# A third block buffer, a mean square taken later, and a longer written order in a sliding-window attention layer

## The chip, the cores and the metric

One core of one Trainium2 chip runs the whole program. The metric is the device time of one execution in microseconds (us), the median of several runs. The core has five instruction streams that run side by side and meet only at semaphores: TensorE (PE; its weight loads are shown as PEld), VectorE (DVE), ScalarE (ACT), GpSimd (POOL) and SyncE (SP, which here only issues DMAs). POOL issues DMAs too, above all the ones that add to what lies at the destination.

## The reference

One layer for 512 tokens of width 2048, all in float32. A root-mean-square norm is followed by a sliding-window attention with 32 heads and its output projection; the result is added to `x`. Then a second norm of `x` feeds a gate, the gate scales an embedding, and a last norm makes the output.

```python
hn = rmsnorm(x, norm_g)
y = swa_mixer(hn, swa_w_in, swa_w_out, swa_sinks, rel_bias)
x = x + y                                        # the kernel's x1
emb = p @ ple_proj
g = jax.nn.sigmoid(rmsnorm(x, ple_norm) @ ple_gate)
x = x + emb * g
return rmsnorm(x, final_g)
# rmsnorm(x, g) = x * rsqrt(mean(x * x) + 1e-6) * g
```

## The kernel before

**Products.** A float32 product is made of three matmuls of a high and a low part (lines 126 to 128). So each block of weights of 128 x 1024 is loaded as `braw` or `grown`, ScalarE copies its high part into `bhi` (line 760), and VectorE subtracts to get the low part `blo` (line 761). Three buffers hold the high parts, three the low ones, and three the raw blocks (a fourth in the last stages). The raw buffer comes free when `blo` has been made, and only then SP's next load (line 752) may start.

**Two large products** follow the attention: the output projection (weights `w_out`, results into `x1`, the four column quarters of `x` after attention) and the gate (weights `ple_gate`). Each is done by a Strassen-like scheme of six large parts in the order 1, 7, 6, 5, 3, 4 (line 669) and some small ones (`smallo`, `smallg`). A part `p` has two halves `jj`, and a half has four steps `m`: 12 matmuls, then some later work, then `todo()` and `between()`. A place in the program is written (p, jj, step) here. The last part of the gate, 4, is written out by hand behind the loop.

**Weights that grow.** In the gate the blocks of parts 7, 6 and 4 share eight buffers `grown`. Each is loaded for part 7; POOL later adds a further block by an accumulating DMA (line 739, always behind the `blo` made from the old contents), which gives the block of part 6, and later that of part 4.

**Turning x1.** The gate's product needs `x1` transposed. Half of it goes over TensorE (`turn`, line 1030). The other half, columns j = 2 and 3 for two halves `th` of the tokens, goes over VectorE (`turn_blocks`, line 1048): two VectorE transposes of 32 x 32 squares into a tile `blocks` with tag "e" and two buffers, a POOL DMA of it to DRAM (`apart`, line 1057), four POOL DMAs that gather it back (line 1064), and four ScalarE instructions that scale it into `hT` (`scale_turned`, line 1066). `turns_at` (line 1075) says at which steps of part 4 of the projection and part 1 of the gate these come. There are four such blocks: (2,0), (3,0), (2,1), (3,1). In their order, the third takes the buffer of the first, and the fourth that of the second.

**The norm.** `squares(t, j)` (line 1025) has ScalarE square a quarter row of `x1`, with the sum kept in `ssq2` and the squares themselves thrown into the scratch tile `s2`. Four of the sixteen are issued where the quarter is complete; twelve are queued in `squares_due` and taken one for each `todo()` from (1,1,0) of the gate on, so that the last comes at (7,1,3). There VectorE sums them (line 1594) and scales the mean (line 1423), POOL raises it to the power -1/2 (line 1425, result `rstd2`), and ScalarE runs one Sigmoid on a single column, which brings in the table for the gates. `rstd2` is first used by `gated` (line 1451), which starts behind step (6,1,1).

**Order.** Inside `tc.manual_schedule(engines=...)` the engines named keep the order in which the program is written; for other engines a planner chooses the order from its own costs. TensorE and SP are always written. ScalarE is written from part 4 of the projection (line 1361) to `last_out.close()` (line 1412), which stands behind the first forms of the gate. In part 1 of the gate ScalarE, VectorE and POOL are the planner's; from part 7 on (line 1560) all engines are written.

Of the kernel before, what the change touches and what calls it, by code (L numbers as in the profile page):

```python
# [11 lines left out]
F32 = mybir.dt.float32  # L12
F32R = mybir.dt.float32r
AF = mybir.ActivationFunctionType
ALU = mybir.AluOpType
AX = mybir.AxisListType
# [4 lines left out]
P = 128  # L21
# [34 lines left out]
def trunk_kernel(ctx: ExitStack, tc: tile.TileContext, a: dict):  # L56
    nc = tc.nc

    def pool(name, bufs=1, **kw):
        return ctx.enter_context(tc.tile_pool(name=name, bufs=bufs, **kw))  # L60
# [25 lines left out]
    WE = 1024  # L86
# [71 lines left out]
    def run(gen):  # L158
        for _ in gen:
            pass  # L160
# [38 lines left out]
    for k in range(KC):  # L199
# [67 lines left out]
        f, e = k == 0, k == KC - 1  # L267
# [18 lines left out]
        for part in "hl" if f else "lh":  # L286
            for t in range(NB):
                c = slice(t * P, (t + 1) * P)
# [6 lines left out]
        if 3 <= k < 3 + NB:  # L295
            t = k - 3
# [104 lines left out]
    for b in range(exact, BUCKETS):  # L401
        d = np.nonzero(bk == b)[0]
        if len(d):
            lo, n = P - 1 + int(d.min()), len(d)
# [301 lines left out]
    for nm, p in SUMS:  # L706
        for q in (6, 5) if (nm, p) == ("ple_gate", 5) else (p,):
            sum_small(nm, q)
        for jj in range(2):
            for m in range(4):  # L710
                t = summed[nm, p, jj, m] = tc.dram_tile([P, WE], F32, name=f"{nm}_{p}_{jj}_{m}")
# [13 lines left out]
    class Pieces:  # L725
# [38 lines left out]
        def split_last(self, k, hi, lo):  # L764

            i = len(self.specs) - 8 + k
            raw = self.base.pop(i)
            nc.scalar.copy(hi, raw)
            nc.vector.tensor_sub(lo, raw, hi.bitcast(F32))
            self.made[i] = tuple([t[:, :512], t[:, 512:]] for t in (hi, lo))  # L770
# [135 lines left out]
    blocks = TWOS * UNITS  # L906
# [64 lines left out]
    late = pool("late", reuse_waits="tile")  # L971
    rooms.append(late)
    x1s = late.tile([P, 4, NB, 512], F32, name="x1s")
    x1 = [x1s[:, j] for j in range(4)]
    ssq2 = const.tile([P, NB, 4], F32, name="ssq2")
# [39 lines left out]
    def load_x(j, queue):  # L1015
        queue.dma_start(x1[j], a["x"].rearrange("(t p) d -> p t d", p=P)[:, :, j * 512 : (j + 1) * 512])

    def partial(nm):
        return late.tile([P, 2, 2, 512], F32, tag="partial", name=nm, bufs=3)

    s1, s2, s7 = partial("s1"), partial("s2"), partial("s7")

    squares_due = []

    def squares(t, j):
        nc.scalar.activation(s2[:, j % 2, t % 2], x1[j][:, t, :], AF.Square, accum_out=ssq2[:, t, j : j + 1])

    hT, swapped = {}, {}

# [17 lines left out]

    def turn_blocks(j, th):

        t = late.tile([P, WE], F32, tag="e", name=f"blocks{j}_{th}", bufs=2)  # L1050
        to = t.rearrange("p (a k t q) -> p t k a q", a=4, k=4, t=2)
        for tb in range(2):
            assert not missing[j, 2 * th + tb]
            src = x1[j][:, 2 * th + tb, :].rearrange("p (k a q) -> p k a q", k=4, a=4)
            nc.vector.transpose(to[:, tb], src)
        apart[j, th] = tc.dram_tile([P, WE], F32, name=f"apart{j}_{th}")
        nc.gpsimd.dma_start(apart[j, th], t)
# [25 lines left out]
    def turns_due(at):  # L1083
        for part, j, th in turns_at.get(at, ()):
            part(j, th)
# [272 lines left out]
    last_out = ExitStack()  # L1358
    for n, p in enumerate(ORDER_OUT):
# [7 lines left out]
        for jj in range(2):  # L1367
# [12 lines left out]
            def todo():  # L1380
                nonlocal fg
                step = next(calls)
                part = x_at.get((p, jj, step))
                if part is not None:
                    load_x(part, nc.sync)
                part = embed_steps.get((p, jj, step))
                if part is not None:
                    embedding.prepare(part)
                next(nxt, None)
                if p == 4:  # L1390
                    turns_due((p, jj, step))
                if (p, jj, step) == (4, 1, 1):
                    fg = late.tile([P, D], F32, tag="fg", name="fg")
                    nc.sync.dma_start(fg, a["final_g"].partition_broadcast(P))
                if (p, jj) == (4, 1):
                    for _ in range(2 if step >= 2 else 0):
                        turn(*turns.pop(0), "o")
                        next(ple_first, None)
# [10 lines left out]
        if p == 3:  # L1409
            turns = [(kp, 0) for kp in range(4)]  # L1410
    run(ple_first)
    last_out.close()
    assert not turns


    power = const.tile([P, NB], F32, name="power")
    nc.gpsimd.memset(power, -0.5)

    def power_of_mean(out, ssq, nm):

        w = out.shape[-1]
        ms = const.tile([P, NB], F32, tag="ms_r", name=f"ms_{nm}")[:, :w]
        nc.vector.tensor_scalar(ms, ssq, 1.0 / D, EPS, op0=ALU.mult, op1=ALU.add)
        yield
        nc.gpsimd.tensor_tensor(out, ms, power[:, :w], op=ALU.pow)

    rstd2 = const.tile([P, NB], F32, name="rstd2")
    ss2 = const.tile([P, NB], F32, tag="sums", name="ss2")
# [4 lines left out]
    def load_embeds(c, jj):  # L1433
        t = embed_of[c, jj] = late.tile([P, 2, 512], F32, tag="e", name=f"e{c}_{jj}", bufs=2)
        nc.sync.dma_start(t, embeds[c, jj])

    def embeds_for(of, which):
        return {t: embed_of[of, which][:, t % 2] for t in ((2, 3) if of == 5 else (0, 1))}
# [91 lines left out]
    def open_bank(jj, tb, tag, c=slice(0, 512)):  # L1530

        ps = opened[jj, tb, c.start] = bank(f"open{jj}_{tb}_{c.start}", tag)
        nc.scalar.mul(ps[:, c], s2[:, jj, tb, c], -1.0)
# [22 lines left out]

    for n, p in enumerate(ORDER_PLE[:-1]):
        if n == 1:

            ctx.enter_context(  # L1560
                tc.manual_schedule(
                    engines={getattr(mybir.EngineType, v) for v in ("PE", "SP", "DVE", "Activation", "Pool")}
                )
            )
        nxt = ple_forms.steps(ORDER_PLE[n + 1])
        for jj in range(2):
            calls = iter(range(4))

            def todo():
                step = next(calls)  # L1570
                k = early.get((p, jj, step))
                if (p, jj, step) in embed_loads:
                    load_embeds(*embed_loads[p, jj, step])
                while small_due:
                    small_due.pop(0)()
                if (p, jj, step) == (5, 0, 2):
                    assert len(moves) == 4
                    while moves:
                        moves.pop(0)()
                if (p, jj, step) == (5, 0, 3):  # L1580
                    for square in moved.pop(0):
                        square()
                if p == 1:
                    turns_due((p, jj, step))
                if turns:
                    turn(*turns.pop(0), "t")
                    return
                next(nxt, None)
                if p == 1:
                    next(nxt, None)  # L1590
                if squares_due:
                    squares_due.pop(0)()
                    if not squares_due:
                        nc.vector.tensor_reduce(ss2, ssq2, axis=AX.X, op=ALU.add)
                        run(power_of_mean(rstd2, ss2, "r2"))
                        nc.scalar.activation(ss2[:, :1], ss2[:, :1], AF.Sigmoid)
                if k is not None:
                    split_last(k)
                if (p, jj, step) in opens:
                    open_bank(*opens[p, jj, step])  # L1600

            def between(m, ps):
                if (p, m) == (7, 3):
                    gate(p, jj, ps, None)
                q = ple_steps.get((p, jj, m))
                if q is not None:
                    small_ple.prepare(q)
                for q in SMALL["ple_gate"].get((p, jj), {}).get(m, ()):
                    small_ple.product(q)
                if (p, jj, m) == (6, 1, 1):  # L1610
                    later.append(partial_of(gate_later, "sum", 0, None, embeds_for(1, 0)))

            ps = unit(p, jj, at_ple, ple_forms, todo, between)
            last_two, held_e = (p, jj) == (3, 1), {}
            if not (p == 7 or last_two):
                later.insert(0, partial_of(gate_later, p, jj, ps, held_e))
            for of, which in EMBEDS.get((p, jj), ()):
                e = embeds_for(of, which)
                held_e.update(e)
                if of == 1:  # L1620
                    later.insert(1, partial_of(gate_later, "sum", which, None, dict(e)))
                    held_e.clear()
            if p == 5:
                while moved:
                    later.extend(moved.pop(0))
        run(nxt)
# [4 lines left out]
    f = ple_forms.made[4]  # L1631
# [84 lines left out]
    n = done[3]  # L1716
# [81 lines left out]
```

## Time and profile before

| | |
|---|---|
| median of 3 runs | 787.8 us (787.77 to 787.85) |
| the profiled execution | 788.14 us, its span 786.4 us |
| TensorE busy | 773.9 us, 98% of the span |
| VectorE, ScalarE, GpSimd busy | 615.6, 528.8, 161.8 us |
| mean granted TensorE clock | 0.996 |
| DMA | 210.92 MB, mean 268 GB/s |

The span runs from the first to the last instruction; 1.74 us of the execution lie around it. A row of the timeline gives start, duration, engine, line, operation, what it writes and reads, and in square brackets how long the engine stood idle before it and what ended that. A row of the windows gives the stretch, its length, the busy time of PE, PEld, DVE, ACT and POOL with the number of instructions that start in it, the granted clock, the DMA engines' busy share (above 1 where transfers of two queues overlap) and GB/s. A row of the waits gives the total, the number and the longest of one kind of wait. A row of DMA issues gives the count, the size of one and the median time from issue to landing.

### The profile page before, as it was taken

The page shows a single profiled execution, that of the slowest core. Times are in us where ns is not written, and L with a number is a line of the kernel's source. Part 1 is how long each engine was busy: PE and PEld are TensorE (multiplying, and loading weights), DVE is VectorE, ACT ScalarE, POOL GpSimd, SP SyncE. Part 2 cuts the span into 40 slices and gives each one's busy share as a digit, 9 for nine tenths or more (in the row PEclk, how much of TensorE's full clock was granted, in tenths as well). Part 3 has the DMA queues.
Part 4 walks back from the last instruction along what each step waited for, and adds up shares of the span by engine and source line. Part 5 has one row for each costly group of instructions (what it writes and reads, how often), then busy time and mean ns, then how long its engine had stood idle before and what let it go on. Part 6 is the DMA issues. An engine that isn't in the chain of part 4 may idle for free.

```text
span 786.4 us, 11162 instructions
## 1 busy us (share of the span) xinstructions
PE 773.9 (98%) x3668; PEld 645.6 (82%) x3668; DVE 615.6 (78%) x1065; ACT 528.8 (67%) x1121; POOL 161.8 (21%) x293
## 2 busy tenths in 40 slices
PE   9999999999999999999999999999999999999995
PEld 8888888888888888888888888888887888887785
DVE  4537697877877688877878898976898879897996
ACT  6734586766767676766666654677675978865974
POOL 0201423132222314132222200001012102221111
PEclk9999999999999999999999999999999999999998
DMA  9988899999999989999997489868799999999956
GB/s 347 286 213 298 188 263 313 291 287 268 276 262 271 273 231 297 276 281 258 288 256 199 139 320 340 263 217 278 242 352 345 261 332 272 223 269 305 303 131 214
DMA packets 51738, 210.92 MB, mean 268 GB/s; under 512 B 7825, under 2 KB 8849, under 8 KB 45921
## 3 DMA queue, kind: packets, MB, share of 16 engines
q1 hardware_dynamic: 39152, 154.58, 56.4%
q0 software_dynamic: 12528, 55.64, 34.5%
q8 instruction: 29, 0.48, 0.2%
q14 instruction: 29, 0.23, 0.1%
HBM read 194.40 MB, written 77.65 MB: 346 GB/s over the span
## 4 chain that ended last, share of the span: by engine, by line
PE 80%; issue 10%; DMA 5%; DVE 3%; POOL 1%; ACT 1%; POOLq 0%; DVEq 0%; ACTq 0%
PE gps L126 7%; PE gps L127 7%; PE gps L128 7%; PE qps L126 7%; PE qps L128 7%; PE qps L127 7%; PE g L127 3%; PE o L127 3%; PE g L128 3%; PE o L126 3%; PE g L126 3%; PE o L128 3%; DMA braw<-ple_gate 3%; PE s L485 2%; DMA apart<-blocks 2%
## 5 line engine op out<-in xcount | busy, mean ns | idle before, releaser
L761 DVE TENSOR_TENSOR blo<-braw,bhi 128x1024 fp32r<-128x1024 f32 x100 | 121.3, 1219 | 24.1 <-ACT bhi L760 23.5
L760 ACT CAST bhi<-braw 128x1024 fp32r<-128x1024 f32 x100 | 105.2, 1053 | 51.2 <-PE o L128 16.5
L126 PE MATMUL gps<-xh,whi 128*128 128x512 f32 x256 | 100.0, 390 | 0.0
L127 PE MATMUL gps<-xl,whi 128*128 128x512 f32 x256 | 99.9, 390 | 0.0
L128 PE MATMUL gps<-xh,wlo 128*128 128x512 f32 x256 | 99.8, 390 | 0.0
L126 PE MATMUL qps<-xh,whi 128*128 128x512 f32 x224 | 87.8, 392 | 0.0
L128 PE MATMUL qps<-xh,wlo 128*128 128x512 f32 x224 | 87.5, 390 | 0.0
L127 PE MATMUL qps<-xl,whi 128*128 128x512 f32 x224 | 87.4, 390 | 0.0
L575 POOL TENSOR_SCALAR_AFFINE_SELECT own<-r 64x512 fp32r<-64x512 f32 (+1 forms) x48 | 32.5, 677 | 238.4 <-DVE r L565 224.4
L110 DVE TENSOR_TENSOR wlo<-wraw,whi 128x1024 fp32r<-128x1024 f32 x60 | 73.5, 1226 | 4.5 <-ACT whi L109 4.4
L126 PE MATMUL o<-bhi,fho 128*128 128x512 f32 x192 | 74.8, 390 | 0.0
L127 PE MATMUL o<-blo,fho 128*128 128x512 f32 x192 | 74.8, 390 | 0.0
L128 PE MATMUL o<-bhi,flo 128*128 128x512 f32 x192 | 74.7, 389 | 0.0
L109 ACT CAST whi<-wraw 128x1024 fp32r<-128x1024 f32 x60 | 62.3, 1040 | 6.3 <-issue 4.1
L127 PE MATMUL g<-blo,fhg 128*128 128x512 f32 x160 | 62.7, 392 | 1.2 <-DVE blo L761 1.2
L126 PE MATMUL g<-bhi,fhg 128*128 128x512 f32 x160 | 62.9, 393 | 0.5 <-ACT bhi L760 0.5
L128 PE MATMUL g<-bhi,flg 128*128 128x512 f32 x160 | 62.4, 390 | 0.0
L128 PEld LDWEIGHTS gps<-xh,wlo 128*128 128x128 f32 x256 | 48.1, 188 | 10.3
L126 PEld LDWEIGHTS gps<-xh,whi 128*128 128x128 f32 x256 | 48.1, 188 | 9.2
L529 ACT ACTIVATE t<-t,sm 128x129 f32<-128x129 f32 (+1 forms) x128 | 49.6, 390 | 8.7 <-DVE sm L525 7.4
L127 PEld LDWEIGHTS gps<-xl,whi 128*128 128x128 f32 x256 | 48.1, 188 | 8.8
L564 ACT CAST r<-pt 128x256 fp32r<-128x256 f32 x56 | 20.9, 372 | 49.8 <-PE pt L551 49.4
(295 smaller groups left out, 1826.2 us busy)
## 6 DMA issues: line engine op xcount, KB each, us to landing
wraw<-in_w_gate_in SPq DMA_DIRECT2D x32, 512.0 KB, 7.7
w_out<-in_w_out POOLq DMA_DIRECT2D x32, 512.0 KB, 9.1
braw<-w_out SPq DMA_DIRECT2D x32, 512.0 KB, 6.6
wraw<-in_w_q SPq DMA_DIRECT2D x28, 512.0 KB, 6.7
braw<-in_w_out SPq DMA_DIRECT2D x22, 512.0 KB, 5.5
braw<-in_ple_gate SPq DMA_DIRECT2D x22, 512.0 KB, 7.0
xw<-in_first SPq DMA_DIRECT2D x14, 640.5 KB, 6.6
w_out<-in_w_out SPq DMA_DIRECT2D x16, 512.0 KB, 10.7
```

The lines of the kernel that those rows point to most:

```text
L109: nc.scalar.copy(hi, raw)
L110: nc.vector.tensor_sub(lo, raw, hi.bitcast(F32))
L126: nc.tensor.matmul(ps, sh, mh, start=first, stop=False, skip_group_check=more)
L127: nc.tensor.matmul(ps, sh, ml, start=False, stop=False, skip_group_check=more)
L128: nc.tensor.matmul(ps, sl, mh, start=False, stop=last, skip_group_check=more)
L485: nc.tensor.matmul(s_ps[:, u, : 2 * n], st, of_keys[:, first * 2 * QB : (first * QB + n) * 2], start=True, stop=True)
L529: nc.scalar.activation(su, su, AF.Exp, bias=sm[:, u : u + 1], accum_out=sm[:, 2 + u : 3 + u])
L564: nc.scalar.copy(rh, src)
L575: nc.gpsimd.affine_select(out=flat(own), in_=flat(r).bitcast(F32), pattern=[[0, 8], [sign, HB]], compare_op=ALU.is_ge, fill=0.0, base=-HB ...
L760: nc.scalar.copy(hi[:, :n], raw)
L761: nc.vector.tensor_sub(lo[:, :n], raw, hi[:, :n].bitcast(F32))
```

## The change

Three edits go together. The third block (2,1) gets room of its own in the first half of the scratch tile `s2`; so that this half is free, all squares go to its second half. The queue of squares starts one step later, at (1,1,1), and takes two at (1,1,3); the sum and the mean move from (7,1,3) to (6,0,1), the power to (6,0,3), and the Sigmoid stays behind the last square but reads `power` in place of the sum. And `last_out.close()` moves behind part 1 of the gate, so that ScalarE's written order runs on through that part.

```diff
@@ squares, line 1025
+    root_due = None
+    ROOT_AT = (6, 0, 1), (6, 0, 3)
 
     def squares(t, j):
-        nc.scalar.activation(s2[:, j % 2, t % 2], x1[j][:, t, :], AF.Square, accum_out=ssq2[:, t, j : j + 1])
+        nc.scalar.activation(s2[:, 1, t % 2], x1[j][:, t, :], AF.Square, accum_out=ssq2[:, t, j : j + 1])
@@ turn_blocks, line 1048
-        t = late.tile([P, WE], F32, tag="e", name=f"blocks{j}_{th}", bufs=2)
+        if (j, th) == (2, 1):
+            t = s2[:, 0].rearrange("p n c -> p (n c)")
+        else:
+            t = late.tile([P, WE], F32, tag="e", name=f"blocks{j}_{th}", bufs=2)
@@ line 1412
     run(ple_first)
-    last_out.close()
@@ the gate's loop, line 1557
     for n, p in enumerate(ORDER_PLE[:-1]):
         if n == 1:
+            last_out.close()
@@ its todo()
-                if squares_due:
+                if (p, jj, step) == ROOT_AT[0]:
+                    assert not squares_due
+                    nc.vector.tensor_reduce(ss2, ssq2, axis=AX.X, op=ALU.add)
+                    root_due = power_of_mean(rstd2, ss2, "r2")
+                    next(root_due)
+                if (p, jj, step) == ROOT_AT[1]:
+                    run(root_due)
+                if squares_due and (p, jj, step) != (1, 1, 0):
                     squares_due.pop(0)()
+                    if (p, jj, step) == (1, 1, 3):
+                        squares_due.pop(0)()
                     if not squares_due:
-                        nc.vector.tensor_reduce(ss2, ssq2, axis=AX.X, op=ALU.add)
-                        run(power_of_mean(rstd2, ss2, "r2"))
-                        nc.scalar.activation(ss2[:, :1], ss2[:, :1], AF.Sigmoid)
+                        nc.scalar.activation(ss2[:, :1], power[:, :1], AF.Sigmoid)
```

More of the change, by code (lines that the diff above doesn't have):

```diff
@@ L1569, in todo @@
             def todo():
+                nonlocal root_due
                 step = next(calls)
```

## The prediction

> **What bounds the kernel now.** I read the page first, then TensorE's waits, then the timeline around each wait. The page says that TensorE sets the time:
>
> ```profile
> PE 773.9 (98%) x3668; PEld 645.6 (82%) x3668; DVE 615.6 (78%) x1065; ACT 528.8 (67%) x1121; POOL 161.8 (21%) x293
> PE smallo L127 <- DVE blo L761: 1.5, 1, 1.5
> PE g L127 <- DVE blo L761: 1.2, 2, 0.8
> PE g L126 <- ACT bhi L760: 0.5, 1, 0.5
> ```
>
> The waits of TensorE are few: one of 1.5 us in the projection and three in the gate. An edit pays only through these, or costs by making new ones. The windows place them and size them by matmul starts:
>
> ```profile
> 590.00:600.00 10.00, 10.00 (x46) 8.29 (x45) 9.79 (x13) 6.57 (x10) 1.05 (x2) 1.00 1.01 308
> 600.00:610.00 10.00, 8.49 (x38) 6.67 (x37) 7.10 (x9) 4.25 (x5) 4.50 (x9) 1.00 1.03 379
> 720.00:730.00 10.00, 8.36 (x33) 5.96 (x33) 8.30 (x11) 8.30 (x14) 1.76 (x2) 1.00 1.07 329
> ```
>
> An undisturbed stretch starts 46 matmuls in 10 us. The stretch from 600 starts 38: stall 1 costs 8/46 x 10 = 1.7 us. That from 720 starts 33: stall 2, with its small stumbles, costs 13/46 x 10 = 2.8 us. Together 4.5 us is all that can be won here.
>
> **Stall 1, and the third buffer.** The timeline around 600:
>
> ```profile
> 577.59 0.54 POOL L1057 DMA_DIRECT2D apart<-blocks  x1 [16.37 <-DVE blo L761]
> ...
> 596.01 0.56 POOL L1057 DMA_DIRECT2D apart<-blocks  x1 [7.47 <-DVE blocks L1055]
> 599.00 1.05 ACT L760 CAST bhi<-braw 128x1024 fp32r<-128x1024 f32 x1 [1.15 <-PE o L128]
> 599.14 0.65 DVE L1147 TENSOR_TENSOR small_alo<-small_sums_o,small_aho 128x512 fp32r<-128x512 f32 x1
> 602.88 0.39 PE L126 MATMUL smallo<-bhi,small_aho 128*128 128x512 f32 x1
> 602.90 0.71 DVE L1055 STREAM_TRANSPOSE blocks<-x1s 128x512 f32<-128x512 f32 x1 [3.11 <-DMA apart<-blocks]
> 603.54 2.32 DVE L761 TENSOR_TENSOR blo<-braw,bhi 128x1024 fp32r<-128x1024 f32 x2
> 604.78 0.50 PE L127 MATMUL smallo<-blo,small_aho 128*128 128x512 f32 x1 [1.51 <-DVE blo L761]
> ```
>
> VectorE stands 3.11 us at the fourth block's transpose, whose buffer is the second block's: that block's DMA, issued at 596.01, is still reading it. Behind the transpose two `blo` are queued, and TensorE, done with the high part at 602.88, needs the first of them. With the third block in `s2`, the fourth takes the first block's buffer. That one's DMA went out at 577.59, some 22 us before the buffer is wanted, against the 3.8 us (596.01 to 599.8) after which the second block's was not yet through. The wait goes. VectorE then transposes at 599.79 (599.14 + 0.65), is done at 600.43, and the `blo`, whose cast ended at 600.05, lasts until about 601.6. TensorE needs it at 602.88 + 0.23 = 603.11, so 1.5 us of margin are left and nothing takes the wait's place: the next thing that could be late is the second `blo`, done at 602.8. I count **-1.7 us**. The transpose, its two halves and its five DMAs stay the same in number.
>
> Does a gain at 604 last to the end? Everything behind is released by TensorE's or VectorE's progress, unless DMA is the limit throughout. It is not: see the idle shares below.
>
> **Stall 2, and the power that is taken later.** Here the loads are late:
>
> ```profile
> 719.57 1.05 ACT L760 CAST bhi<-braw 128x1024 fp32r<-128x1024 f32 x1 [2.86 <-DMA braw<-ple_gate]
> 725.92 1.05 ACT L760 CAST bhi<-braw 128x1024 fp32r<-128x1024 f32 x1 [0.65 <-DMA braw<-ple_gate]
> e<-embeds SPq DMA_DIRECT2D x1, 512.0 KB, 4.6
> braw<-ple_gate SPq DMA_DIRECT2D x1, 512.0 KB, 12.7
> 700.00:710.00 10.00, 10.00 (x46) 8.29 (x45) 8.22 (x10) 5.49 (x7) 3.00 (x4) 1.00 1.06 275
> ```
>
> ScalarE waits for `braw` before the casts that TensorE lacks. The DMA issues by short windows show why: a load of 512 KB issued between 676 and 678 lands in 4.6 us, one issued between 712 and 714 in 12.7 us, with the DMA engines' share above 1 between. Transfers queue up. Where the queue starts:
>
> ```profile
> 670.23 1.22 DVE L761 TENSOR_TENSOR blo<-grown,bhi 128x1024 fp32r<-128x1024 f32 x1
> 673.17 1.22 DVE L761 TENSOR_TENSOR blo<-grown,bhi 128x1024 fp32r<-128x1024 f32 x1
> 676.43 1.23 DVE L761 TENSOR_TENSOR blo<-grown,bhi 128x1024 fp32r<-128x1024 f32 x1 [0.91 <-ACT bhi L760]
> 678.02 1.06 POOL L1425 TENSOR_TENSOR rstd<-ms_r,power 128x4 f32<-128x4 f32 x1 [10.10 <-DVE ms_r L1423]
> 679.05 2.71 POOL L739 DMA_DIRECT2D grown<-in_ple_gate  x3
> 674.00:676.00 2.00, 2.00 (x10) 1.68 (x9) 1.52 (x2) 0.96 (x3) 0.00 (x0) 1.00 0.59 229
> 676.00:678.00 2.00, 2.00 (x10) 1.65 (x10) 1.48 (x3) 1.98 (x4) 0.00 (x0) 1.00 0.73 154
> 678.00:680.00 2.00, 2.00 (x11) 1.65 (x10) 1.13 (x2) 1.99 (x5) 1.98 (x3) 1.00 0.90 367
> 680.00:682.00 2.00, 2.00 (x11) 1.65 (x10) 1.74 (x3) 1.43 (x2) 1.77 (x2) 1.00 0.77 90
> ```
>
> POOL stands 10.10 us at the power of the mean square. Behind it three accumulating DMAs are queued, which then go out together at 679.05. What they themselves wait for, the `blo` of their buffers, ended at 671.5, 674.4 and 677.7. While they stand, the DMA engines are partly idle: 0.41, 0.27, 0.10 and 0.23 of four stretches of 2 us, **2.0 us** in all. With the power written at (6,0,3) these three go out as their `blo` ends, fill that idle time, and the queue that follows is 2.0 us of transfer shorter when it reaches 720. Bounds: 0, if the late loads do not depend on it, and the whole 2.8 us of stall 2, because the loads would also meet fewer accumulating transfers. I take 2.0, the idle time that the rows show: **-2.0 us**. The power itself (1.06 us on POOL) stands in the new place before later adds; its input is two steps old by then, and the power is needed first when `gated` starts behind (6,1,1).
>
> ```profile
> 677.57 0.16 DVE L1594 TENSOR_REDUCE ss<-ssq 128x4 f32<-128x16 f32 x1
> 677.77 0.17 DVE L1423 TENSOR_SCALAR ms_r<-ss 128x4 f32<-128x4 f32 x1
> 690.00:700.00 10.00, 10.00 (x46) 8.29 (x45) 10.00 (x12) 6.80 (x8) 2.12 (x3) 1.00 1.05 270
> ```
>
> The sum and the mean (0.16 + 0.17 us of VectorE) move from 677.6, where VectorE had idle time near by, to (6,0,1), which lies in the stretch up to 700 where VectorE has none. They delay the `blo` behind them, and so the release of raw buffers: **+0.3 us** at most, 0 if TensorE's cover holds. I take 0.3. The Sigmoid reads another column, and ScalarE pays for it as before.
>
> A rule would speak against the -2.0. The Trainium skill ("DMA: Bandwidth & Descriptors", section on the anatomy of one SWDGE DMA) fits a DMA as 2.0 us plus its bytes at 436 GB/s; as an estimate from that page, 512 KB take 3.2 us, and 275 GB/s would be far from full. The trace disagrees as far as it goes, with 12.7 us for such a load at a share above 1; the rival below prices the case.
>
> **ScalarE's written order in part 1.**
>
> ```profile
> L1026 ACT ACTIVATE s<-x1s x16: 621/628/649, 539.7 to 676.3; 128x512 f32<-128x512 f32 x16
> 571.64 0.63 ACT L1026 ACTIVATE s<-x1s 128x512 f32<-128x512 f32 x1
> 620.00:630.00 10.00, 10.00 (x54) 8.36 (x53) 8.45 (x11) 10.00 (x20) 0.00 (x0) 1.00 0.83 211
> 630.00:640.00 10.00, 10.00 (x49) 8.27 (x48) 7.84 (x10) 10.00 (x21) 0.00 (x0) 1.00 0.82 288
> 640.00:650.00 10.00, 10.00 (x46) 8.27 (x45) 6.82 (x7) 5.67 (x7) 0.93 (x1) 1.00 1.01 397
> ```
>
> The planner had pulled the four squares of part 1 forward, to 571 and on, into the projection. Now they run where they are written, about 640 to 650: 4 x (0.63 + 0.19) = 3.3 us at most. ScalarE has 10 - 5.67 = 4.3 us free there, so they are hidden, with 1.0 us to spare. From 620 to 640 it has none, and the written order puts some casts one step of the turning later; the casts run two blocks ahead of TensorE (2 x 12 matmuls x 0.22 = 5.2 us, less 1.05 for the cast and 1.2 for `blo`: 3 us of cover). Cost 0; without cover up to the 2.3 us of one cast and one `blo`. The squares leave 571, but VectorE, not ScalarE, is the full engine there (9.79 of 10 before 600), so that gives nothing. Idle DMA shares of 0.17 and 0.18 from 620 to 640 show that the DMA backlog of the projection is worked off here; this is why stall 1's gain is not lost again.
>
> **Sum.** -1.7 - 2.0 + 0.3 = -3.4 us. The profiled execution took 788.14 us (span 786.4, 1.74 around it), so it would take 784.7; it lies 0.3 above the median of 787.8, from which the same sum gives **784.4 us**.
>
> **Rivals.**
>
> *Stall 2 stays* (the loads are late for another reason; by the skill's fit DMA has headroom). For it: only 275 GB/s in 700 to 710, where 640 to 650 moved 397. Against it: the share of 1.06, the landing times. -1.7 + 0.3 gives 786.4.
>
> *Stall 1's gain is not kept*: TensorE comes 1.7 us earlier and stands 1.7 us longer at 720, because transfers set the pace from 640 on. For it: shares above 1 in most of that time. Against it: the idle 2.0 us at 674 to 682. -2.0 + 0.3 gives 786.1.
>
> *Slower: VectorE waits for TensorE in place of the DMA.* VectorE's order in the projection's last part is the planner's, and it is in order and full there. Freed of the buffer, the planner may put a block's transposes with the add that they read ahead of the `blo` of the next products. Then VectorE stands until TensorE has finished the product, and TensorE afterwards until the add (0.68), two transposes (1.4) and two `blo` (2.3) are done: 4.3 us each time. Both late blocks so: 2 x 4.3 - 1.7 (stall 1) - 1.7 (the gain at 720) = +5.2, or 793.0. It is slower by over 0.2% once these new stalls reach 1.7 + 1.7 + 1.6 = 5.0 us. Against it: before, transposes follow the adds without such a stall.
>
> *It does nothing*: the transpose finds another wait as long, and the adds another reason to stand: 787.8.
>
> **Chances.** Forecast 0.56; stall 2 stays 0.15; stall 1's gain not kept 0.13; slower 0.12; nothing 0.04. A measurement of this kernel tells about 0.2% (1.6 us, so 786.2 and 789.4) from no change. The two middle cases lie by that edge: I count 0.12 of their 0.28 as faster and 0.16 as no difference. Faster 0.68, same 0.20, slower 0.12. The range goes from both stalls gone and no cost, -4.5 or 783.3 with 0.3 for the runs, to the case of nothing but part of one gain: 783.0 to 787.4.
>
> **What would show it.** In the new profile VectorE's wait before the `blocks` transpose is gone and 600 to 610 starts 46 matmuls. POOL's accumulating DMAs near 670 to 678 each follow their `blo`, the power comes near 690 after no long wait, DMA shares of 674 to 682 rise to about 1, loads at 712 land faster than 12.7 us, and TensorE's waits for `g` shrink to under 1 us. I am wrong if VectorE waits for a `smallo` or `o` before a `blo`, if ScalarE makes TensorE wait between 620 and 650, or if the loads at 712 take as long as before.

## The result, and the profile after

The changed kernel takes **783.6 us** (783.42 to 783.81 in six runs) against 787.83 us (787.27 to 789.13) for the kernel before on the same chip: a ratio of 0.9943, 95% interval 0.9931 to 0.9956. The profiled execution took 783.81 us with a span of 781.7 (before: 788.14 and 786.4).

First TensorE's waits, the view that set the argument (total, number, longest). The waits for `smallo` and for `g` that the prediction shows are gone. What is left is one at the program's start, which the kernel before has too (0.8 us):

```profile
PE warm_ps L141 <- PEq L1801: 0.9, 1, 0.9
```

The windows of the changed kernel, in the same columns as before: the stretches of both stalls start 46 matmuls each, with TensorE busy all 10 us. ScalarE from 640 is at 9.70 of 10, where four squares now run, and TensorE loses nothing. Below, the four stretches in which the DMA engines had stood idle by 0.41, 0.27, 0.10 and 0.23; they are full.

```profile
600.00:610.00 10.00, 10.00 (x46) 8.29 (x45) 8.11 (x9) 5.51 (x6) 2.73 (x5) 1.00 1.01 328
640.00:650.00 10.00, 10.00 (x46) 8.29 (x45) 8.66 (x10) 9.70 (x18) 1.80 (x2) 1.00 1.06 393
720.00:730.00 10.00, 10.00 (x46) 8.29 (x45) 8.75 (x11) 8.24 (x13) 1.76 (x2) 1.00 1.04 341
...
674.00:676.00 2.00, 2.00 (x11) 1.65 (x10) 1.23 (x1) 2.00 (x4) 0.00 (x0) 1.00 1.05 215
676.00:678.00 2.00, 2.00 (x11) 1.65 (x10) 0.88 (x2) 1.99 (x5) 0.85 (x1) 1.00 1.07 238
678.00:680.00 2.00, 2.00 (x11) 1.65 (x10) 1.74 (x3) 1.68 (x2) 0.00 (x0) 1.00 1.01 317
680.00:682.00 2.00, 2.00 (x10) 1.68 (x9) 2.00 (x3) 1.28 (x2) 0.58 (x1) 1.00 1.08 285
```

The timeline of POOL around the power, and of VectorE around 600. From 670 to 677 each accumulating DMA now follows its own `blo`; the power at 686.10 comes after the adds and stands 3.83 us for the mean, and two adds go out behind it. The fourth block's transpose at 599.28 has no wait in front of it.

```profile
670.01 0.86 POOL L739 DMA_DIRECT2D grown<-in_ple_gate  x1 [3.82 <-DVE blo L761]
672.95 0.85 POOL L739 DMA_DIRECT2D grown<-in_ple_gate  x1 [2.08 <-DVE blo L761]
676.22 0.85 POOL L739 DMA_DIRECT2D grown<-in_ple_gate  x1 [2.42 <-DVE blo L761]
...
686.10 1.43 POOL L1429 TENSOR_TENSOR rstd<-ms_r,power 128x4 f32<-128x4 f32 x1 [3.83 <-DVE ms_r L1427]
687.50 1.81 POOL L739 DMA_DIRECT2D grown<-in_ple_gate  x2
...
599.28 0.70 DVE L1060 STREAM_TRANSPOSE blocks<-x1s 128x512 f32<-128x512 f32 x1
600.26 1.23 DVE L761 TENSOR_TENSOR blo<-braw,bhi 128x1024 fp32r<-128x1024 f32 x1 [0.27 <-ACT bhi L760]
```

One thing in the new timelines was not in the prediction. The third block is turned some 55 us earlier than before (at 595 to 599 then): as soon as its quarter of `x1` is complete, and its gathering follows.

```profile
540.67 1.30 DVE L1060 STREAM_TRANSPOSE s<-x1s 128x512 f32<-128x512 f32 x2
...
542.27 0.53 POOL L1062 DMA_DIRECT2D apart<-s  x1 [1.42 <-DVE s L1060]
558.11 1.14 POOL L1069 DMA_DIRECT2D s<-apart  x2 [1.06 <-DVE x1s L1103]
```

VectorE and POOL are the planner's in that part. What had held this block back was the buffer. In this kernel the early turn hurts nothing; the experiments show when it does.

### The profile page after: what moved, and what is told of

Its sections match the earlier page's. It is cut to its first block, busy times and chain, and to the rows that moved or that the text cites. A ratio compares the mean times of both kernels' runs of the same rounds, so it can differ in the third digit from the quotient of the medians.

```text
span 781.7 us, 11153 instructions
## 1 busy us (share of the span) xinstructions
PE 772.4 (99%) x3668; PEld 646.3 (83%) x3668; DVE 615.9 (79%) x1065; ACT 529.1 (68%) x1121; POOL 161.8 (21%) x293
## 4 chain that ended last, share of the span: by engine, by line
PE 98%; issue 1%; DVE 0%; POOL 0%; POOLq 0%; DVEq 0%
PE gps L126 7%; PE gps L127 7%; PE gps L128 7%; PE qps L126 7%; PE qps L128 7%; PE qps L127 7%; PE o L128 6%; PE o L127 6%; PE o L126 6%; PE g L128 5%; PE g L127 5%; PE g L126 5%; PE s L485 2%; PE vps L290 2%; PE o L603 2%; PE pt L551 2%
```

## The experiments

Three edits went together, so the runs first take each combination of them. "Lost starts" counts, in the stretches of 10 us in which TensorE is busy for less than 10 (they lie in 570 to 590, 600 to 610 and 710 to 730), by how many matmuls each falls short of 46; one is worth 10/46 = 0.22 us. They are counted in the one profiled execution of each kernel.

| third buffer | late power | longer written order | median us | ratio to before, 95% | lost starts |
|---|---|---|---|---|---|
| no | no | no | 787.83 (the kernel before) | 1 | 8 + 13 = 21 |
| yes | no | no | 788.27 | 0.9996 (0.9983 to 1.0009) | 8 + 2 + 12 = 22 |
| no | no | yes | 787.96 | 1.0008 (0.9994 to 1.0023) | 6 + 2 + 12 = 20 |
| yes | no | yes | 786.48 | 0.9969 (0.9958 to 0.9981) | 7 + 7 = 14 |
| no | yes | no | 785.12 | 0.9957 (0.9942 to 0.9971) | 8 |
| yes | yes | no | 785.91 | 0.9972 (0.9960 to 0.9984) | 6 + 3 = 9 |
| no | yes | yes | 784.42 | 0.9944 (0.9926 to 0.9963) | 5 |
| yes | yes | yes | 783.60 (the changed kernel) | 0.9943 (0.9931 to 0.9956) | 0 |

The rows were timed in four sessions and not all on one chip. In these sessions the kernel before had medians of 787.83, 788.47, 787.76 and 787.88, and each ratio compares with the kernel before in the same session. So differences between rows of under about 1 us rest on the lost starts more than on the clock: by their ratios the last two rows can't be told apart.

### Undo the third buffer

```diff
-        if (j, th) == (2, 1):
-            t = s2[:, 0].rearrange("p n c -> p (n c)")
-        else:
-            t = late.tile([P, WE], F32, tag="e", name=f"blocks{j}_{th}", bufs=2)
+        t = late.tile([P, WE], F32, tag="e", name=f"blocks{j}_{th}", bufs=2)
```

> The changed kernel with the third block back in the tag e, so that the fourth again takes the second's buffer; the rest as changed. My theory: VectorE stands about 3 us at the fourth block's transpose, TensorE 1.5 us behind it, and the time is 783.6 + 1.7 = 785.3. Rival (the stall went because the squares left ScalarE's earlier stretch, or by the new order): no such wait, 783.6.

784.42 us (783.72 to 785.60). The timeline of VectorE:

```profile
602.60 0.71 DVE L1057 STREAM_TRANSPOSE blocks<-x1s 128x512 f32<-128x512 f32 x1 [2.35 <-DMA apart<-blocks]
```

The windows:

```profile
600.00:610.00 10.00, 9.26 (x41) 7.34 (x40) 7.65 (x10) 4.73 (x5) 4.38 (x8) 1.00 1.03 378
```

Stall 1 is back at its place and with its releaser, but at 5 starts (1.1 us) in place of 8, behind a stand of 2.35 us in place of 3.11. With the written order, the fourth transpose meets a DMA that is nearer its end. Why it is nearer was not tried.

### Undo the late power

```diff
-                if (p, jj, step) == ROOT_AT[0]:
...
-                    run(root_due)
...
                     if not squares_due:
-                        nc.scalar.activation(ss2[:, :1], power[:, :1], AF.Sigmoid)
+                        nc.vector.tensor_reduce(ss2, ssq2, axis=AX.X, op=ALU.add)
+                        run(power_of_mean(rstd2, ss2, "r2"))
+                        nc.scalar.activation(ss2[:, :1], ss2[:, :1], AF.Sigmoid)
```

> The changed kernel with sum, mean and power back at (7,1,3), right behind the last square. My theory: POOL stands about 10 us at the power, three accumulating DMAs go out together, DMA is partly idle before, and TensorE waits for late loads near 715: 783.6 + 2.8 = 786.4, or 785.6 if only the 2.0 us of idle DMA time count. Rival (the loads are late for another reason, or the gain came by the order of ScalarE): 783.6.

786.48 us (786.24 to 787.25). The timeline of POOL shows the stand of 10.10 us, and three adds out together behind it:

```profile
676.03 1.05 POOL L1429 TENSOR_TENSOR rstd<-ms_r,power 128x4 f32<-128x4 f32 x1 [10.10 <-DVE ms_r L1427]
677.06 2.71 POOL L739 DMA_DIRECT2D grown<-in_ple_gate  x3
```

The windows show 14 starts lost (7 and 7, 3.0 us) some 40 us later:

```profile
710.00:720.00 10.00, 8.72 (x39) 6.66 (x37) 7.12 (x9) 4.06 (x6) 0.00 (x0) 1.00 1.06 285
720.00:730.00 10.00, 9.61 (x39) 7.14 (x40) 8.94 (x12) 8.02 (x13) 1.75 (x2) 1.00 1.06 346
```

### Undo the longer written order

```diff
     run(ple_first)
+    last_out.close()
...
         if n == 1:
-            last_out.close()
```

> The changed kernel with last_out.close() back ahead of part 1 of the gate, so that the planner orders ScalarE there again. My theory: the written order neither costs nor brings anything, 783.6. Rival (the written order earns a part): 784.5 or more; other rival (it costs, hidden in the total): under 783.0.

785.91 us (785.59 to 787.16): here my theory was wrong. Stall 1 is gone and stall 2 is gone (46 starts from 600 and from 720), but there is a new stall between 570 and 590. The windows:

```profile
570.00:580.00 10.00, 9.24 (x40) 6.93 (x38) 7.65 (x10) 7.95 (x15) 0.56 (x1) 1.00 1.02 378
580.00:590.00 10.00, 9.90 (x43) 7.79 (x43) 10.00 (x14) 6.12 (x7) 2.19 (x4) 1.00 0.94 278
```

The timeline of ScalarE has its cause:

```profile
568.18 1.05 ACT L760 CAST bhi<-braw 128x1024 fp32r<-128x1024 f32 x1
571.70 1.71 ACT L1078 ACTIVATE hT<-s,pn 128x256 f32<-128x256 f32 x4 [2.48 <-DMA s<-apart]
573.32 1.03 ACT L760 CAST bhi<-braw 128x1024 fp32r<-128x1024 f32 x1
```

This is the third block's scaling, written at (1,0,1) of the gate, where it runs at 626 in the changed kernel:

```profile
626.22 1.71 ACT L1078 ACTIVATE hT<-s,pn 128x256 f32<-128x256 f32 x4
```

(A row does not name its block. ScalarE is in written order there, and its four scalings start at 611.01, 615.10, 626.22 and 632.61, so the third is this one.) With ScalarE planned in part 1, and the block gathered early, the planner brought it forward by some 55 us. There it stands 2.48 us for the gathering DMA and then runs 1.71 us, and the cast that TensorE needs is queued behind it. What the stand and the work cost each by itself was not tried.

### The third buffer alone

The kernel before with the first two hunks of the diff only: the block's room in `s2`, and the squares in its other half.

> The kernel before with the third buffer alone. My theory: the first stall goes and the second stays, 787.8 - 1.7 = 786.1. Rival (transfers set the pace from 640 on, so TensorE stands longer at 720 for what it won): 787.8.

788.27 us (787.60 to 789.38): no gain. The timeline of ScalarE, VectorE and TensorE:

```profile
571.67 1.71 ACT L1076 ACTIVATE hT<-s,pn 128x256 f32<-128x256 f32 x4 [2.84 <-DMA s<-apart]
573.29 1.03 ACT L760 CAST bhi<-braw 128x1024 fp32r<-128x1024 f32 x1
574.35 1.22 DVE L761 TENSOR_TENSOR blo<-braw,bhi 128x1024 fp32r<-128x1024 f32 x1 [2.38 <-ACT bhi L760]
575.63 0.50 PE L127 MATMUL smallo<-blo,small_aho 128*128 128x512 f32 x1 [0.76 <-DVE blo L761]
```

The windows:

```profile
570.00:580.00 10.00, 9.11 (x38) 6.60 (x36) 7.28 (x11) 7.93 (x15) 0.56 (x1) 1.00 1.00 373
580.00:590.00 10.00, 9.90 (x44) 7.82 (x43) 10.00 (x14) 6.14 (x7) 2.19 (x4) 1.00 0.93 284
600.00:610.00 10.00, 10.00 (x46) 8.29 (x45) 8.63 (x10) 5.05 (x5) 2.74 (x5) 1.00 1.02 358
720.00:730.00 10.00, 8.48 (x34) 5.96 (x33) 8.29 (x11) 7.89 (x14) 1.75 (x2) 1.00 1.07 332
```

The number was that of my rival, for another reason than the rival's. The transpose's wait is gone as foretold (46 from 600). A new one of 8 + 2 starts, 2.2 us, took its place 30 us earlier. It can be followed row by row: scaling late, cast behind it, `blo` behind the cast (2.38 us idle), matmul behind the `blo`. Stall 2 is there as before.

### The late power alone

The kernel before with only the sum and the mean at (6,0,1) and the power at (6,0,3); the squares start at (1,1,0) as before.

> The kernel before with the sum and mean at (6,0,1) and the power at (6,0,3) alone. My theory: the second stall goes and the first stays, 787.8 - 2.8 = 785.0 (785.8 if the idle DMA time of 2.0 us is all). Rival (it needs TensorE's earlier arrival or the written order too): 787.8.

785.12 us (784.18 to 787.66), as expected. Stall 1 is there in full, stall 2 has gone:

```profile
600.00:610.00 10.00, 8.51 (x38) 6.70 (x37) 6.90 (x9) 4.26 (x5) 4.44 (x9) 1.00 1.03 387
720.00:730.00 10.00, 10.00 (x46) 8.26 (x45) 9.92 (x13) 8.53 (x14) 1.76 (x2) 1.00 1.05 356
```

### The sum at once, the power late

```diff
                     if not squares_due:
+                        nc.vector.tensor_reduce(ss2, ssq2, axis=AX.X, op=ALU.add)
+                        root_due = power_of_mean(rstd2, ss2, "r2")
+                        next(root_due)
-                        nc.scalar.activation(ss2[:, :1], power[:, :1], AF.Sigmoid)
+                        nc.scalar.activation(ss2[:, :1], ss2[:, :1], AF.Sigmoid)
```

(The same three lines are taken out at (6,0,1), and the Sigmoid reads the sum again, as in the kernel before. The rest is the changed kernel.)

> The changed kernel with VectorE's sum and mean back at (7,1,3) and only POOL's power at (6,0,3). My theory (POOL's stand alone makes the second stall): 783.6, no waits of TensorE for g. Rival (VectorE's two instructions at 677 hold the blo behind them): 786.4 or a part of it.

783.63 us (783.35 to 784.22), no wait of TensorE. So VectorE's two small instructions cost the same in both places, nothing that shows. With the mean early, POOL takes the power at 681.59 without the stand of 3.83 us that the changed kernel has there, and that gains nothing that shows either.

### POOL held on purpose

To hold POOL without touching the norm, the changed kernel got one more power on POOL at (7,1,3), whose result goes into a small tile `held` that nothing uses.

```diff
                     if not squares_due:
+                        nc.gpsimd.tensor_tensor(held, ssq2[:, :, 0], power, op=ALU.pow)
                         nc.scalar.activation(ss2[:, :1], power[:, :1], AF.Sigmoid)
```

> The changed kernel with one more POOL instruction at (7,1,3): a power of four sums that nobody reads, which has to wait for the last square. VectorE and ScalarE do what they do in the changed kernel. My theory: POOL stands about 10 us, the three accumulating DMAs go out together and the second stall is back: 786.4, or 785.6 if only 2.0 us count. Rival: 783.6, with only the 1.1 us of POOL more.

782.97 us (782.65 to 783.95). The theory's stall did not come, but the theory was not put to the test: the column that it reads is not the last to be squared, so POOL stood for 2.90 us only. One add went out behind it at 669.69, some 0.9 us after its `blo` had ended at 668.80 (timeline of POOL):

```profile
668.18 1.54 POOL L1610 TENSOR_TENSOR held<-ssq,power 128x4 f32<-128x4 f32 x1 [2.90 <-ACT s L1028]
669.69 0.92 POOL L739 DMA_DIRECT2D grown<-in_ple_gate  x1
```

What the run does show is that one more power on POOL costs nothing by itself: its ratio of 0.9936 (0.9919 to 0.9953) can't be told from the changed kernel's. The second try reads the column that is squared last, `ssq2[:, :, 1]`:

> The changed kernel with an extra power on POOL at (7,1,3) that reads the sums of the last column of squares, so that POOL waits there for the last square; its result is not used. Theory (what cost 2.8 us was that POOL, in order, stood in front of three accumulating DMAs): POOL stands some 9 us until about 676, the three DMAs go out together, TensorE starts fewer than 46 matmuls between 710 and 730, 786.4 us. Rival (the mean and power themselves, or where their other instructions stand, made the difference): 783.6 us as the changed kernel.

785.46 us (784.95 to 786.22; ratio 0.9966, 0.9951 to 0.9980). The timeline of POOL:

```profile
674.72 1.47 POOL L1610 TENSOR_TENSOR held<-ssq,power 128x4 f32<-128x4 f32 x1 [9.18 <-ACT s L1028]
676.17 2.69 POOL L739 DMA_DIRECT2D grown<-in_ple_gate  x3
```

The windows:

```profile
710.00:720.00 10.00, 9.24 (x40) 7.13 (x39) 7.49 (x10) 4.99 (x7) 0.00 (x0) 1.00 1.06 288
720.00:730.00 10.00, 9.59 (x41) 7.12 (x40) 8.94 (x12) 7.98 (x13) 1.73 (x2) 1.00 1.05 357
```

Here the mean and the power stay late, and stall 2 comes back with 11 lost starts (2.4 us) and 1.9 us in the medians. With the run before this one as the control, it is the stand that does it. It is a little shorter than that of before (9.18 for 10.10 us), and so is the stall.

The DMA issues say how it gets from 676 to 720. For the kernel before, the changed one and this one, the two rows of each are the adds issued from 668 to 692 and the plain loads issued from 700 to 720 (count, size, median us to landing):

```profile
grown<-in_ple_gate POOLq DMA_DIRECT2D x6, 512.0 KB, 12.8
braw<-ple_gate SPq DMA_DIRECT2D x6, 512.0 KB, 11.1
```

```profile
grown<-in_ple_gate POOLq DMA_DIRECT2D x7, 512.0 KB, 8.6
braw<-ple_gate SPq DMA_DIRECT2D x5, 512.0 KB, 8.1
```

```profile
grown<-in_ple_gate POOLq DMA_DIRECT2D x7, 512.0 KB, 13.0
braw<-ple_gate SPq DMA_DIRECT2D x5, 512.0 KB, 11.3
```

Where three adds go out together, adds take 13 us, and the loads that start 30 us later still take 3 us longer; where they go out one by one, both land in some 8 us.

### The written order alone

The kernel before with only `last_out.close()` moved.

> The kernel before with only the written order of ScalarE run on to the end of part 1; two buffers, power at (7,1,3). Theory (the written order pays only as a guard against the third block's scaling being pulled forward, and with two buffers the buffer holds it back anyway): 787.1 us, that is the 0.7 us by which two buffers with the late power and the written order were below the late power alone, and a short wait of VectorE left at 602. Rival (the written order is worth 1.8 to 2.3 us by itself): 785.7 us.

787.96 us (786.52 to 790.90): no gain by itself, neither the theory's 0.7 us nor the rival's 1.8 to 2.3. Stall 1 is a little shorter (windows; 40 starts from 600 for 38), and stall 2 is unchanged in size and begins a little earlier:

```profile
600.00:610.00 10.00, 8.96 (x40) 7.08 (x39) 7.76 (x10) 4.53 (x5) 4.41 (x8) 1.00 1.03 368
...
710.00:720.00 10.00, 9.78 (x44) 7.74 (x42) 6.63 (x8) 4.55 (x6) 0.00 (x0) 1.00 1.05 279
720.00:730.00 10.00, 8.62 (x34) 6.34 (x35) 8.18 (x11) 7.71 (x14) 1.75 (x2) 1.00 1.07 334
```

### The written order as far as the scaling

The changed kernel with `last_out.close()` right behind the third block's scaling. The four squares of part 1 go forward into the projection again, as before the change; the scaling does not.

```diff
                 step = next(calls)
+                if (p, jj, step) == (1, 0, 2):
+                    last_out.close()
...
         if n == 1:
-            last_out.close()
```

> The changed kernel with the written order of ScalarE ended right behind the third block's scaling, at (1,0,2), in place of the end of part 1. The four squares of part 1 are the planner's again and go forward into the projection. Theory (the stall at 570 to 590 in the planned order comes from the scaling that waits for its gather on ScalarE): the scaling stays near 610, TensorE starts 46 matmuls in each 10 us from 570 to 610, 783.6 us. Rival (the squares pulled forward, or ScalarE's full load there, make the stall): 785.9 us.

783.82 us (783.43 to 784.13; ratio 0.9948, 0.9928 to 0.9967), no wait of TensorE. The timeline of ScalarE has the squares early and the third block's scaling at 627, close to its 626 in the changed kernel (the 610 of the expectation is where the first block's runs):

```profile
571.45 0.63 ACT L1028 ACTIVATE s<-x1s 128x512 f32<-128x512 f32 x1
...
626.89 1.72 ACT L1078 ACTIVATE hT<-s,pn 128x256 f32<-128x256 f32 x4
```

The window from 570, where the planned order had lost 6 starts, has TensorE busy for all 10 us:

```profile
570.00:580.00 10.00, 10.00 (x45) 8.28 (x45) 10.00 (x14) 8.29 (x13) 0.56 (x1) 1.00 1.02 394
```

So of the longer written order, the part that counts reaches only as far as the third block's scaling: it keeps these four instructions behind the projection's casts. Where the squares run is worth nothing that shows, in either place.

## Why the prediction was right, and where it was not

The forecast of 784.4 us lies 0.8 us above the 783.6 measured; of its steps one held in full, one was too small, one was nothing, and one was right only with an edit that it had valued at nothing.

**What bounds the kernel** held. TensorE's lost starts account for the time: 21 x 0.22 = 4.6 us in the profile before, 4.2 us gained when all are gone; and over the table, the lost starts follow the medians within half a microsecond (22 starts, 4.8 us, for 4.7 over the changed kernel; 14, 3.0, for 2.9; 9, 2.0, for 2.3; 5, 1.1, for 0.8).

**Stall 2, -2.0: right mechanism, too small.** The four pairs of the table that differ in the late power give -2.7 (787.83 to 785.12), -2.4, -3.5 and -2.9 us. The idle DMA time of 2.0 us was the wrong measure; the upper bound, all 2.8 us of the stall, was the right one. The idle share counts when the DMA engines stand, not how little they move while they are busy. From 680 to 688, behind the three adds, the kernel in which POOL stands (the second try) moved 216 and 220 GB/s at shares of 1.05 and 1.02; the changed kernel moved 277 and 288 at 1.05 and 1.06. From 668 to 692 the kernel in which POOL stands moved 5.62 MB and the changed kernel 6.75. At the 273 GB/s that the first of them moved next (692 to 700), the 1.13 MB between them are some 4 us of transfer, an estimate, where the idle share gave 2.0. The prediction's reason for the upper bound, that the loads also meet fewer adds at once, fits the landing times above, but no run separates it from the shorter queue. The rival that stall 2 stays is excluded by the same pairs. It had leaned on the Trainium skill's "DMA: Bandwidth & Descriptors", section on the anatomy of one SWDGE DMA; its 3.2 us for 512 KB, an estimate from that page, was not met by these DMAs in either kernel, as adds landed in 12.8 and 8.6 us. That section is about DMAs that GpSimd issues, as these adds are; the 12.7 us that the prediction set against it was a load on SP's queue.

**The sum and the mean, +0.3: nothing.** Putting them back gave 783.63. VectorE's cover held. But the power's input was not "two steps old": POOL came to the power first and stood 3.83 us until the mean, written two steps earlier, ended on VectorE at 686.0. The first of the two adds behind it, whose `blo` ended at 684.0, so went out 3.5 us late, at no cost that shows.

**Stall 1, -1.7: right place, incomplete reason.** The wait at the transpose went, with the releaser named and with nothing in its place there. But the time is won only together with the written order, so the step that failed is that "nothing takes the wait's place": the prediction looked for a successor near 602, and without the written order one came at 570 to 590. With that order, the buffer gains 1.5 us (787.96 to 786.48) or, the power being late, 0.8 (784.42 to 783.60, which rests on the 5 starts); without it, +0.4 and +0.8 us, no gain. The transpose, its halves and its DMAs did "stay the same in number", but not in place. The buffer had also been what kept the block's whole chain of turn, gathering and scaling late.

**The written order, 0: wrong as a term.** I asked only what it costs and where the squares go, and compared it with the order of before. Its value lies against the order that the planner would choose once the buffer is there: 1.8 us (788.27 to 786.48) and 2.3 us (785.91 to 783.60). Without the third buffer it is +0.1 and -0.7. That the change held it all the same, without a gain being asked of it, was luck for the term of stall 1. The hiding of the squares behind ScalarE's 4.3 free us was right.

**The slower rival** was near the truth and on the wrong engine. The planner did take its new freedom and did make TensorE wait; but it was on ScalarE, for a gathering DMA, and for 2.2 us in place of 8.6. The longer written order keeps that from happening, and I had not connected the two. **Stall 1's gain not kept** did not come: once all three are there, no stretch between is short. Nor does stall 2 take it where it stays: with the written order but the early power, the buffer removes the 6 starts lost from 600, and the stretches from 710 to 730 lose 14 with it and without it.

So the total came out near though three terms were off. Two errors add up: 0.8 us too little for stall 2 and a cost of 0.3 that did not come. A third takes a part of them back: with 2.8 of the 4.2 us gained for stall 2, some 1.4 are left for stall 1 in place of 1.7.

## What to carry to other kernels

A buffer that is waited for can also be what keeps an instruction in its place: before adding one, ask what a planner will pull forward on every engine down the chain, and which in-order queue will then stand behind a DMA; fix that part of the order by hand. An engine that both computes and issues DMAs should not wait for a late operand in front of them: here 10 us of standing on an engine that is 21% busy cost TensorE 2.8 us, 40 us later. And counting the starts that are missing in short windows of the bounding engine gave the worth of each edit to about half a microsecond.

## What the runs showed that was not expected

How long a backlog of transfers lasts: a stand of POOL of 9 to 10 us near 670, which sends three adds out some 3 to 8 us after their `blo` has ended, makes loads issued at 700 to 720 land in 11.1 or 11.3 us in place of 8.1, though the kernels move the same blocks. And ScalarE has little slack for one wrong instruction in the projection's last part: a stand of 2.5 to 2.8 us with 1.7 us of work behind it cost TensorE 2.0 to 2.2 us, while four squares between 571 and 592, 0.6 us each and without a wait, cost nothing.
